# Conditioning columns off two projections' ends, the second block's shifts on VectorE, and the step widths' chain behind a convolution's taps

## The chip, the cores and the metric

The kernel runs as one program on one core of one Trainium2 chip. Its time is the device time of one execution in microseconds (us). TensorE (PE, matrix products), VectorE (DVE), ScalarE (ACT), GpSimd (POOL) and the queue of SyncE (SP), which issues the transfers, each run their own instruction stream in order and meet at semaphores. A stream that waits holds up all that stands behind it in the same stream.

## The reference, cut to what matters

Three blocks follow each other on 256 tokens of width 1024. The first has two layers (a state space mixer with a gated short convolution, then attention), each with a gated feed-forward network; the second is one recurrent mixer with a mixture of 32 experts; the third is an attention block. The diff touches three computations: the step widths `dt` of the state space mixer, the modulation rows `mod` that condition blocks two and three, and the shifted projections, decays and recurrence of the second block's mixer.

```python
# block 1, layer 1
xbc = silu(causal_dwconv(xbc, conv_w) + conv_b)
dt = softplus(dt_raw + dt_bias)
da = dt * -exp(a_log)
a_cs = cumsum(da)                      # decays follow from it
# block 2 (block 3 likewise, three parts of its own)
mod = silu(c) @ ada_w[l] + ada_b[l]
shift1, scale1, gate1, shift2, scale2, gate2 = split(mod, 6)
# block 2, mixer
zs = z + (z_prev - z) * mu             # token_shift; r, k, v are parts of zs
log_decay = -exp(-softplus(-w_pre) - 0.5)
kk = k * k_k / max(norm(k * k_k), eps)
k = k * (1 + (a - 1) * k_a)
for t in tokens:                       # per head
    state = state * w_t - (state @ kk_t) (kk_t * a_t)^T + v_t k_t^T
    y_t = state @ r_t
```

The kernel computes the recurrence in chunks of 128 tokens, which needs products of the decays with k, kk and r and the inverse of a triangular matrix for each chunk and head.

## The kernel before, in words

**Projections.** `dense_F` multiplies the 256 tokens by a weight matrix. Weights come as raw tiles through SP's queue and are worked off in units of 128 x 1024. Each unit is split into a high part `wh` (a rounded copy on ACT, line 338) and a low part `wl` (the difference, line 342, on DVE; every third unit of the first block's larger matrices on POOL). PE then runs 24 products of 128 x 256 for a unit: `xh*wh`, `xl*wh`, `xh*wl`, for eight groups. Units are split three ahead of PE (two ahead in the second block's mixer), and there are four buffers of `wh` and `wl` (three in the mixer). Four accumulators `acc` hold results.

**Background work.** Everything that isn't a projection is written as generators in one queue (`push`). `tick` runs the next piece of the first of them, and `dense_F` calls it once a unit. So the order in which all engines see the pieces is settled when the program is built: a piece stands, in every engine's stream, behind the splits of the units that were issued before it. `drain` runs what is left.

**Step widths.** After the 16 columns of `dt_raw` are projected, `widths` (line 868) transposes them on PE (L875), runs a softplus on DVE and ACT (L876 to L889, with Exp at L879 and Ln at L882), forms `da` (L890), and a tick later runs two products with it and two Exp (L896, L897). Before, it is pushed ahead of `conv(8)`, the first of three convolutions. Each convolution pushes 12 taps on DVE (L811) and a Silu on ACT (L814). `consts2` then builds masks on DVE and POOL.

**Conditioning columns.** One column of `mod` is one DVE instruction over a 128 x 1024 tile `adat` of transposed `ada_w` (`cond`, L1274), which multiplies by `silu(c)` and sums. There are 56 columns, and three `adat` buffers. Each column, when it is done, issues the transfer of a later column's tile (`cond_load`, L1291). `MODS[i]` says how many columns are pushed at which place in layer i's feed-forward network: entry 2q after gate product q, entry 2q+1 after up product q (q from 0 to 5), entry 11 + k/4 at unit k of the down product. The residual `sg` of gate and up is multiplied at L1161, split at L594, and the down product reads it.

**Second block's mixer.** `shift` (L1390) forms token-shifted r, k and v: one difference, on POOL for the wide ones (L1392), then four fused multiply-adds on DVE (L1394). `k_chain` and `r_chain` multiply them with decays (`KR` at L1462 and L1477, `v["k"]` with `E2` at L1478). In `rwkv`, `invert` solves 15 steps on DVE for each half t (L1693 to L1697), `Tm` is formed from it (L1780), and `corner` (L1771) masks `AB` on POOL. Four transposes per group (L1787) and products follow.

Of the kernel before, what the change touches and what calls it, by code (L numbers as in the profile page):

```python
# [33 lines left out]
T = 256  # L34
# [112 lines left out]


EXPERTS = [(1, 0)] + [x for e in range(31) for x in ((1, e + 1), (2, e))] + [(2, 31)]
MODS = [[0, 3] + [2] * 9 + [3] + [0] * 6, [0, 3] + [2] * 9 + [3] + [3, 3, 2, 0, 0, 0]]  # L150


def weight_plan(stages):
# [271 lines left out]
class KB:  # L425
# [351 lines left out]
    def ssd_layer(self, xf):  # L777
        nc, pp = self.nc, self.pp
        es = ExitStack()
        P = es.enter_context(self.pool("ssd", 1))  # L780
        X = self.xpool

        warm = self.tl(pp, [128, 128], F32, "tp")
        for _ in range(8):
            self.mm(warm, self.ident, self.ident, start=True)
        self.st.ahead(1)
        x = self.resplit(xf, X)

        def padded(n):
            pad = self.tl(P, [128, 4, T + 3], F32, "pad", bufs=2)  # L790
            nc.gpsimd.memset(pad[:, :, 0:3], 0.0)
            return pad


        xs = self.tl(P, [128, 8, T], F32, "xs")
        bc = self.tl(P, [128, 4, T], F32, "bc")

        def conv(c0):
            ps = self.dense_F("w_in_mix", x)
            pad = padded(4)  # L800
            dst = xs[:, c0:c0 + 4] if c0 < 8 else bc
            for j in range(4):
                if j % 2 == 0:
                    nc.scalar.activation(pad[:, j:j + 2, 3:], ps[j // 2], AF.Copy)
                nc.scalar.activation(dst[:, j], ps[j // 2][:, j % 2], AF.Identity, bias=self.col("conv_b", c0 + j),
                                     scale=self.col("conv_w", 36 + c0 + j))

            def taps():
                for j in range(4):
                    for tap in range(3):  # L810
                        nc.vector.scalar_tensor_tensor(dst[:, j], pad[:, j, tap:tap + T], self.col("conv_w", 12 * tap + c0 + j),  # L811
                                                       dst[:, j], op0=OP.mult, op1=OP.add)
                    yield
                nc.scalar.activation(dst, dst, AF.Silu)  # L814

            self.push("conv", taps())

        self.x_done = False
        ps = self.dense_F("w_in_mix", x, n=16)
        dr = self.tl(P, [16, T], F32, "dr")  # L820
        nc.scalar.activation(dr, ps[0][0:16, 0], AF.Copy)
        v = {}
        self.push("widths", self.widths(P, dr, v))
        conv(8)
        self.push("consts", self.consts2())
        conv(0)
        conv(4)
        self.push("states", self.state_space(P, xs, bc, v))

        z = self.z = self.tl(P, [128, 8, T], F32, "z")  # L830
        for h in range(2):
            ps = self.dense_F("w_in_mix", x)
            for j in range(2):
                s = slice(4 * h + 2 * j, 4 * h + 2 * j + 2)
                nc.scalar.activation(z[:, s], ps[j], AF.Silu)

        self.pad(P, 16)
        sx = (self.tl(P, [128, 8, T], F32R, "sch"), self.tl(P, [128, 8, T], F32R, "scl"))
        for h in range(2):
            cc = self.tl(P, [128, 4, T], F32, "cc")  # L840
            ps = self.dense_F("w_in_mix", x)
            for j in range(2):
                nc.scalar.activation(cc[:, 2 * j:2 * j + 2], ps[j], AF.Copy)
            ps = self.dense_F("w_in_mix", x)
            pad = padded(4)
            for j in range(2):
                nc.vector.tensor_mul(pad[:, 2 * j:2 * j + 2, 3:], cc[:, 2 * j:2 * j + 2], ps[j])
            for j in range(4):
                c = h * 4 + j
                nc.scalar.activation(cc[:, j], pad[:, j, 3:3 + T], AF.Copy, scale=self.col("sc_w", 16 + c))  # L850
                for tap in range(2):
                    nc.vector.scalar_tensor_tensor(cc[:, j], pad[:, j, 1 + tap:1 + tap + T], self.col("sc_w", 8 * tap + c),
                                                   cc[:, j], op0=OP.mult, op1=OP.add)
            ps = self.dense_F("w_in_mix", x)
            for j in range(2):
                s = slice(2 * j, 2 * j + 2)
                nc.vector.tensor_mul(cc[:, s], cc[:, s], ps[j])
                so = slice(4 * h + 2 * j, 4 * h + 2 * j + 2)
                self.split(cc[:, s], sx[0][:, so], sx[1][:, so])
        self.x_done = True  # L860
        ps = self.residual(xf)
        self.rows_T("w_out_mix", sx, 0, 8, ps)
        self.drain()
        r = self.rows_norm("w_out_mix", self.yx, 8, ps, "lnm", 0, self.cond_fill(0))
        es.close()
        return r
# [485 lines left out]
    def mixer(self, xf, stat):  # L1352
        nc, pp, st = self.nc, self.pp, self.st
# [11 lines left out]
        c4 = lambda ap: ap.rearrange("p j (t s) -> p j t s", s=128)  # L1365
# [23 lines left out]

        def shift(pad, mu0, n, dst):  # L1390

            (nc.gpsimd if n > 2 else nc.vector).tensor_sub(dst, pad[:, 0:n, 0:T], pad[:, 0:n, 1:])  # L1392
            for j in range(n):
                nc.vector.scalar_tensor_tensor(dst[:, j], dst[:, j], self.col("mu", mu0 + j), pad[:, j, 1:],  # L1394
                                               op0=OP.mult, op1=OP.add)

        KR = self.tl(P, [128, 4, 2, 2, 128], F32, "KR")
        bz = self.tl(P, [128, 2, 4, T], F32, "bz")
        ta, sig, cs, E1, g = t4("d"), t4("a"), t4("b"), t4("c"), t4("e")
        E0, E2 = sig, cs  # L1400
        hs = self.tl(P, [128, 4], F32, "hs")
        v = {}
# [41 lines left out]
        def k_chain(pad):  # L1444
            zk = v["k"] = t4("f")
            shift(pad, 4, 4, zk)
            yield
            kap, sq = t4("h"), t4("i")
            for j in range(4):
                nc.vector.tensor_scalar(kap[:, j], zk[:, j], self.col("k_k", j), None, op0=OP.mult)  # L1450
            nc.scalar.activation(sq, kap, AF.Square)
            yield
            rs = self.head_rsqrt(sq, P, 1.0, 1e-24, OP.max)
            yield
            for j in range(4):
                nc.vector.tensor_mul(kap[:, j], kap[:, j], self.head_row(rs, j))

            f = t4("i")
            for j in range(4):
                nc.scalar.activation(f[:, j], ta[:, j], AF.Identity, bias=hk[:, 1, j:j + 1], scale=hk[:, 0, j:j + 1])  # L1460
            yield
            nc.gpsimd.tensor_mul(KR[:, :, :, 0], c4(kap), c4(E0))  # L1462
            nc.vector.scalar_tensor_tensor(ta, ta, 1.0, kap, op0=OP.add, op1=OP.mult)
            nc.vector.tensor_mul(zk, zk, f)
            yield

            for e in range(2):
                nc.vector.scalar_tensor_tensor(bz[:, e], ta, hm[:, e:e + 1], E2, op0=OP.mult, op1=OP.mult)
            yield

        def r_chain(pad):
            zr, sq = t4("h"), t4("i")
            shift(pad, 0, 4, zr)
            yield
            for j in range(4):
                nc.vector.scalar_tensor_tensor(sq[:, j], zr[:, j], self.col("r_k", j), v["k"][:, j], op0=OP.mult, op1=OP.mult)
            nc.vector.tensor_mul(KR[:, :, :, 1], c4(zr), c4(E1))  # L1477
            nc.gpsimd.tensor_mul(v["k"], v["k"], E2)  # L1478
            v["bonus"] = sq
            yield  # L1480

# [32 lines left out]
        pad = padded(ps, 2)  # L1514
# [116 lines left out]
    def rwkv(self, P, P2, KR, bz, kh, V, hs, stick):  # L1631
# [136 lines left out]
        TT = self.tl(P, [128, 2, 8, 128], F32, "bz")  # L1768
        Al = {}

        def corner(lev, t):  # L1771
            Al[t] = self.tl(P, [128, 8, 128], F32, "pad", bufs=2)
            nc.gpsimd.tensor_mul(Al[t], units(AB[:, t, :, :, 0:128]), self.corners[:, lev, None, :].to_broadcast([128, 8, 128]))

        for t in range(2):
            corner(0, t)
        for t in range(2):
            for _ in inv[t]:
                pass
            nc.vector.tensor_mul(  # L1780
                Tm[:, t].rearrange("p u (b s) -> p u b s", s=16), Tc[:, t, :, None, :].to_broadcast([128, 8, 8, 16]),
                self.blk16.rearrange("p (b s) -> p b s", s=16)[:, None].to_broadcast([128, 8, 8, 16]))
        for t in range(2):
            for h in range(2):
                p = self.tl(pp, [128, 4, 128], F32, "tp")
                for u in range(4):
                    nc.tensor.transpose(p[:, u], Tm[:, t, 4 * h + u], self.ident)  # L1787
                nc.scalar.activation(TT[:, t, 4 * h:4 * h + 4], p, AF.Copy)
            fill()
# [842 lines left out]
```

## Time and profile before

| | us |
|---|---|
| three executions | 2259.61, 2260.05, 2253.85 |
| their median | 2259.61 |
| the profiled execution | 2253.87 |
| its span, first to last instruction | 2252.1 |
| PE busy in it | 2122.8 (94%) |
| DVE, ACT, POOL busy | 1073.3, 724.5, 269.1 |

The mean granted clock of PE was 0.974 of its full speed. The profile gives busy time by engine and by 40 slices of the span, then groups of instructions by line. The trace can be asked for the waits of an engine, for a stretch of the timeline, and for the busy time in given windows. In a timeline row the first number is the start in us from the start of the span, the second the duration; a bracket at its end gives the idle time of the engine just ahead and what ended it. A row with "x6" is a run of six instructions of one kind.

### The profile page before, as it was taken

Reading aid. Unit: us, or ns where it says so; the run is one execution under the profiler, and the core shown is the slowest. Engines: PE = TensorE matmul, PEld = TensorE weight load, DVE = VectorE, ACT = ScalarE, POOL = GpSimd, SP = SyncE. Lnnn points to the kernel's source line nnn. Section 1 sums busy time; section 2 is a strip of 40 time slices with the busy share of each in tenths; the row PEclk is TensorE's granted clock in tenths of the full one; section 3 lists DMA queues with packets and bytes.
Section 4 is the critical chain, followed back from the end, with each engine's and each line's share of the span. In section 5 each row is a group of like instructions: output and inputs, shape, how many; then the busy total and the mean of one; then the engine's idle time right before and its main releaser. Section 6 shows DMA issues by size and latency. Waiting matters only on the chain. (4 is left out here: it accounts for less than half of the span.)

```text
span 2252.1 us, 31704 instructions
## 1 busy us (share of the span) xinstructions
PE 2122.8 (94%) x13258; PEld 1489.4 (66%) x13258; DVE 1073.3 (48%) x2013; ACT 724.5 (32%) x1169; POOL 269.1 (12%) x144
## 2 busy tenths in 40 slices
PE   8999999999999988799899999999999999999996
PEld 8997997887997878688444444334433333368886
DVE  6775775566787567746222222322221111245665
ACT  5444543554543454343111110111111111133552
POOL 2322232100232012310000000000000000004101
PEclk9999999999999999999899999999999999999999
DMA  7334785332787433105799999999999999984320
GB/s 295 150 146 158 309 315 206 152 150 86 312 319 271 176 122 113 38 1 219 324 426 427 427 423 427 427 428 427 427 428 427 428 427 427 427 333 161 119 76 20
DMA packets 65652, 618.06 MB, mean 274 GB/s; under 512 B 8128, under 2 KB 10176, under 8 KB 19808
## 3 DMA queue, kind: packets, MB, share of 16 engines
q1 hardware_dynamic: 62320, 612.33, 66.5%
q10 hardware_dynamic: 3184, 3.65, 0.5%
q8 instruction: 106, 1.74, 0.3%
q14 instruction: 42, 0.34, 0.0%
HBM read 614.90 MB, written 1.05 MB: 274 GB/s over the span
## 5 line engine op out<-in xcount | busy, mean ns | idle before, releaser
L555 PE MATMUL acc<-xh,wh 128*128 128x256 f32 (+1 forms) x1736 | 487.5, 285 | 7.3 <-ACT wh L338 2.8
L555 PE MATMUL acc<-xl,wh 128*128 128x256 f32 (+1 forms) x1736 | 482.2, 281 | 2.9 <-DVE xl L594 1.5
L555 PE MATMUL acc<-xh,wl 128*128 128x256 f32 (+2 forms) x1704 | 476.4, 280 | 5.3 <-DVE wl L342 5.3
L555 PE MATMUL acc<-expert,xe 128*64 128x512 f32 x2000 | 447.7, 598 | 17.7 <-DMA expert<-exp_w 17.7
L342 DVE TENSOR_TENSOR wl<-w,wh 128x1024 fp32r<-128x1024 f32 x202 | 270.1, 1346 | 155.3 <-ACT wh L338 154.8
L338 ACT ACTIVATE wh<-w 128x1024 fp32r<-128x1024 f32 (+1 forms) x263 | 274.0, 1054 | 213.7 <-PE acc L555 176.0
L555 PEld LDWEIGHTS acc<-xh,wh 128*128 128x128 f32 (+1 forms) x1736 | 326.5, 189 | 16.2 <-issue 5.6
L555 PEld LDWEIGHTS acc<-expert,xe 128*64 128x64 f32 x2000 | 140.5, 137 | 294.8 <-issue 275.5
L555 PEld LDWEIGHTS acc<-xl,wh 128*128 128x128 f32 (+1 forms) x1736 | 328.8, 191 | 7.5 <-DVE xl L594 3.5
L555 PEld LDWEIGHTS acc<-xh,wl 128*128 128x128 f32 (+2 forms) x1704 | 322.5, 189 | 7.1 <-DVE wl L342 6.9
L555 PE MATMUL py<-expert,aT 128*64 128x512 f32 x1024 | 234.3, 600 | 3.6 <-DMA expert<-exp_w 2.8
L342 POOL TENSOR_TENSOR wl<-w,wh 128x1024 fp32r<-128x1024 f32 (+1 forms) x61 | 153.4, 2515 | 527.6 <-ACT wh L338 468.4
L2069 ACT ACTIVATE s<-a 128x512 f32<-128x512 f32 x32 | 20.2, 630 | 530.1 <-DVE a L2068 530.1
L2136 DVE SCALAR_TENSOR_TENSOR xf<-py,mod,xf 128x256 f32<-128x256 f32 x128 | 55.7, 479 | 279.8 <-PE py L555 279.8
L2068 DVE TENSOR_SCALAR a<-acc 128x512 f32<-128x512 f32 x32 | 22.1, 692 | 346.2 <-PE acc L555 346.2
L555 PEld LDWEIGHTS py<-expert,aT 128*64 128x64 f32 x1024 | 72.0, 138 | 137.3 <-issue 127.8
L342 POOL TENSOR_TENSOR wl<-w_w_in,wh 128x1024 fp32r<-128x1024 f32 (+1 forms) x11 | 26.8, 2435 | 1053.8 <-ACT wh L338 1042.9
L1274 DVE SCALAR_TENSOR_TENSOR adat<-adat,pe 128x1024 f32<-128x1024 f32 x56 | 97.3, 1756 | 12.3 <-DMA adat<-tiles 12.3
L2123 ACT ACTIVATE y<-py 64x512 f32<-64x512 f32 x64 | 37.9, 592 | 117.9 <-PE py L555 117.4
L555 PE MATMUL tp<-sel,xh 128*128 128x128 f32 x512 | 63.3, 284 | 7.9 <-ACT aT L2103 6.9
L555 PE MATMUL acc<-wh,hh 128*128 128x512 f32 x176 | 69.7, 396 | 0.0
L555 PE MATMUL acc<-wl,hh 128*128 128x512 f32 x176 | 69.4, 394 | 0.0
(641 smaller groups left out, 2856.2 us busy)
## 6 DMA issues: line engine op xcount, KB each, us to landing
expert<-exp_w SPq DMA_DIRECT2D x188, 2048.0 KB, 31.3
w<-tiles SPq DMA_DIRECT2D x140, 1024.0 KB, 6.9
adat<-tiles SPq DMA_DIRECT2D x56, 512.0 KB, 7.7
w_w_in<-tiles SPq DMA_DIRECT2D x18, 1024.0 KB, 5.0
w<-exp_w SPq DMA_DIRECT2D x3, 2048.0 KB, 7.6
w_w_out<-tiles SPq DMA_DIRECT2D x4, 1024.0 KB, 4.8
expert<-exp_w SPq DMA_DIRECT2D x4, 512.0 KB, 30.1
w_w_o_moba<-tiles SPq DMA_DIRECT2D x2, 1024.0 KB, 4.7
```

The costliest lines, as they stand in the source:

```text
L338: kb.nc.scalar.activation(hi, w, AF.Copy)
L342: (kb.nc.gpsimd if far else kb.nc.vector).tensor_sub(lo, w, hi.bitcast(F32))
L555: self.nc.tensor.matmul(out, lhsT, rhs, start=start, stop=True, skip_group_check=True)
L1274: self.nc.vector.scalar_tensor_tensor(w, w, 1.0, crow[:, int(m >= 48)], op0=OP.mult, op1=OP.mult, accum_out=dst)
L2068: nc.vector.tensor_scalar(a, pg, 7.0, None, op0=OP.min)
L2069: nc.scalar.activation(s, a, AF.Sigmoid, scale=1.702)
L2123: nc.scalar.activation(y[r, o], py[r], AF.Copy)
L2136: nc.vector.scalar_tensor_tensor(xf[:, k], ps[o][:, c], gate2(k), xf[:, k], op0=OP.mult, op1=OP.add)
```

## The change

Four places are edited. The step widths' generator is pushed behind the first convolution's taps. The table `MODS` has three columns instead of two after gate 2, up 3 (and the same in layer 2), none after gate 5 and up 5, and three at unit 4 of the down product (layer 2: 3, 3, 3, 2 from there). The wide shift differences, the first half of `KR` and the product of k with `E2` go from POOL to DVE. The first two of the `corner` masks go from POOL, ahead of the inversion's last steps, to DVE, right behind each `Tm`.

```diff
-MODS = [[0, 3] + [2] * 9 + [3] + [0] * 6, [0, 3] + [2] * 9 + [3] + [3, 3, 2, 0, 0, 0]]
+MODS = [[0, 3, 2, 2, 3, 2, 2, 3, 2, 2, 0, 0] + [3] + [0] * 5, [0, 3, 2, 2, 3, 2, 2, 3, 2, 2, 0, 0] + [3, 3, 3, 2, 0, 0]]
...
         v = {}
+        conv(8)
         self.push("widths", self.widths(P, dr, v))
-        conv(8)
         self.push("consts", self.consts2())
...
-            (nc.gpsimd if n > 2 else nc.vector).tensor_sub(dst, pad[:, 0:n, 0:T], pad[:, 0:n, 1:])
+            nc.vector.tensor_sub(dst, pad[:, 0:n, 0:T], pad[:, 0:n, 1:])
...
-            nc.gpsimd.tensor_mul(KR[:, :, :, 0], c4(kap), c4(E0))
+            nc.vector.tensor_mul(KR[:, :, :, 0], c4(kap), c4(E0))
...
-            nc.gpsimd.tensor_mul(v["k"], v["k"], E2)
+            nc.vector.tensor_mul(v["k"], v["k"], E2)
...
-        def corner(lev, t):
+        def corner(lev, t, engine=nc.gpsimd):
             Al[t] = self.tl(P, [128, 8, 128], F32, "pad", bufs=2)
-            nc.gpsimd.tensor_mul(Al[t], units(AB[:, t, :, :, 0:128]), self.corners[:, lev, None, :].to_broadcast([128, 8, 128]))
-
-        for t in range(2):
-            corner(0, t)
+            engine.tensor_mul(Al[t], units(AB[:, t, :, :, 0:128]), self.corners[:, lev, None, :].to_broadcast([128, 8, 128]))
+
         for t in range(2):
             for _ in inv[t]:
                 pass
             nc.vector.tensor_mul(
...
+            corner(0, t, nc.vector)
```

What this does to the instruction streams is shown at three places. The numbers behind names count tiles as the program makes them, and differ between the two kernels.

ACT, from the first units of layer 1's input projection, kernel before:

```order
L821 ACTIVATE dr_189<-acc_149 16x256
L338 ACTIVATE wh_193<-w_1_76 128x1024
L879 ACTIVATE dw_37_225<-dw_37_225 128x32
L880 ACTIVATE na_231<-rows_96 128x16
L882 ACTIVATE dw_39_227<-dw_38_226 128x32
L338 ACTIVATE wh_250<-w_4_79 128x1024
L896 ACTIVATE dte_230<-tp_278 128x16
L897 ACTIVATE ea_229<-tp_278 128x16
```

The same four lines of the step widths in the changed kernel, now behind the Silu of the first convolution:

```order
L338 ACTIVATE wh_455<-w_3_78 128x1024
L814 ACT_TABLE_LOAD
L814 ACTIVATE bc_148<-bc_148 128x1024
L879 ACT_TABLE_LOAD
L879 ACTIVATE dw_59_488<-dw_59_488 128x32
L880 ACTIVATE na_494<-rows_96 128x16
L882 ACT_TABLE_LOAD
L882 ACTIVATE dw_61_490<-dw_60_489 128x32
L338 ACTIVATE wh_513<-w_5_154 128x1024
L896 ACT_TABLE_LOAD
L896 ACTIVATE dte_493<-tp_541 128x16
L897 ACTIVATE ea_492<-tp_541 128x16
```

The chain now has a table load ahead of its Exp, another ahead of its Ln and a third ahead of the later Exp; ACT's stream has four loads more in all, the fourth ahead of a later Silu (L835). On PE the two products with `da` stand 192 products, eight units, later than before.

DVE, at the end of layer 1's up product, where the residual is multiplied (L1161), kernel before:

```order
L1274 SCALAR_TENSOR_TENSOR adat_3580,mod_15_119<-adat_3580,pe_2344 128x1024
L342 TENSOR_TENSOR wl_3745<-w_30_3297,wh_3744 128x1024
L1274 SCALAR_TENSOR_TENSOR adat_3611,mod_15_119<-adat_3611,pe_2344 128x1024
L1274 SCALAR_TENSOR_TENSOR adat_3708,mod_15_119<-adat_3708,pe_2344 128x1024
L1161 TENSOR_TENSOR sg_3741<-sg_3741,acc_3743 128x512
L594 TENSOR_TENSOR hl_2349<-sg_3741,hh_2348 128x512
L342 TENSOR_TENSOR wl_3830<-w_30_3297,wh_3829 128x1024
```

The same place in the changed kernel:

```order
L1274 SCALAR_TENSOR_TENSOR adat_3586,mod_15_119<-adat_3586,pe_2344 128x1024
L342 TENSOR_TENSOR wl_3751<-w_30_3300,wh_3750 128x1024
L1161 TENSOR_TENSOR sg_3747<-sg_3747,acc_3749 128x512
L594 TENSOR_TENSOR hl_2349<-sg_3747,hh_2348 128x512
L342 TENSOR_TENSOR wl_3830<-w_30_3300,wh_3829 128x1024
L342 TENSOR_TENSOR wl_3849<-w_31_3429,wh_3848 128x1024
```

The two columns that stood between the last `wl` and L1161 are gone from there; three stand some units later, in the down product.

DVE, at the end of the inversion of the first half, kernel before:

```order
L1695 TENSOR_REDUCE k_9059<-k_9059 128x8
L1697 TENSOR_SCALAR k_9059<-k_9059,idc_596 128x8
L1780 TENSOR_TENSOR kz_9369<-k_9059,blk_77_599 128x1024
L1697 TENSOR_SCALAR k_9059<-k_9059,idc_596 128x8
L1693 TENSOR_TENSOR k_9059<-k_9059,bz_9178 128x8x12
```

The same place in the changed kernel, whose lines there have numbers lower by two:

```order
L1695 TENSOR_REDUCE k_9059<-k_9059 128x8
L1697 TENSOR_SCALAR k_9059<-k_9059,idc_624 128x8
L1778 TENSOR_TENSOR kz_9369<-k_9059,blk_79_627 128x1024
L1773 TENSOR_TENSOR pad_9373<-AB_9046,corners_628 128x1024
L1697 TENSOR_SCALAR k_9059<-k_9059,idc_624 128x8
L1693 TENSOR_TENSOR k_9059<-k_9059,bz_9178 128x8x12
```

The corner mask stands between the first half's `Tm` (L1780, now L1778) and the rest of the second half's inversion.

## Rows read from the trace of the kernel before

**Rows 1.** Page, busy us by engine (share of the span, instructions):

```profile
PE 2122.8 (94%) x13258; PEld 1489.4 (66%) x13258; DVE 1073.3 (48%) x2013; ACT 724.5 (32%) x1169; POOL 269.1 (12%) x144
```

**Rows 2.** Waits of PE: tile, line waited for: us, times, longest:

```profile
PE acc L555 <- DVE sg L1161: 11.1, 2, 5.6
...
PE tp L1497 <- DVE k L1394: 4.0, 1, 4.0
PE tp L1787 <- DVE k L1697: 3.7, 1, 3.7
...
PE tp L555 <- DVE da L890: 3.0, 1, 3.0
```

**Rows 3.** Windows: us, busy by engine (instructions), granted clock, DMA share, GB/s:

```profile
23.00:26.25 3.25, 3.25 (x17) 3.25 (x16) 0.00 (x0) 0.56 (x1) 2.38 (x2) 0.50 1.02 416
26.25:58.50 32.25, 32.25 (x286) 32.25 (x286) 27.37 (x58) 22.71 (x32) 9.78 (x9) 1.00 0.56 220
358.70:364.20 5.50, 5.48 (x17) 4.71 (x18) 4.21 (x6) 1.58 (x2) 0.00 (x0) 0.50 0.51 171
695.80:699.00 3.20, 3.19 (x12) 2.95 (x13) 2.29 (x3) 1.57 (x2) 0.00 (x0) 0.54 0.48 165
957.40:964.50 7.10, 7.07 (x25) 5.22 (x25) 5.68 (x17) 2.52 (x5) 0.00 (x0) 0.50 0.00 0
```

**Rows 4.** Timeline, end of layer 1's up product, DVE and PE:

```profile
356.83 1.23 DVE L1274 SCALAR_TENSOR_TENSOR adat<-adat,pe 128x1024 f32<-128x1024 f32 x1 [3.71 <-DMA adat<-tiles]
...
357.98 0.68 DVE L1161 TENSOR_TENSOR sg<-sg,acc 128x512 f32<-128x512 f32 x1
...
358.72 1.65 PE L555 MATMUL acc<-alphaI,xf 128*128 128x128 f32 x6 [5.61 <-DVE sg L1161]
```

**Rows 5.** Tile `adat`, 255 to 375 us, its 21 transfers:

```profile
DMA to landing us min/median/max: 3.5/7.7/10.4
```

**Rows 6.** Timeline, layer 1's input projection, ACT, DVE and PE:

```profile
18.58 0.23 ACT L879 ACTIVATE dw<-dw 128x32 f32<-128x32 f32 x1 [2.92 <-DVE dw L878]
...
20.70 0.19 DVE L890 SCALAR_TENSOR_TENSOR da<-dt,na 128x32 f32<-128x32 f32 x1
...
42.26 1.28 ACT L814 ACT_TABLE_LOAD   x1
...
43.55 1.06 ACT L814 ACTIVATE bc<-bc 128x1024 f32<-128x1024 f32 x1
...
60.69 0.39 PE L555 MATMUL acc<-xh,wl 128*128 128x256 f32 x1 [1.71 <-DVE wl L342]
```

**Rows 7.** Timeline, second block's mixer, PE and DVE:

```profile
843.91 2.16 PE L555 MATMUL tp<-heads,i 128*128 128x2 f32 x16 [2.07 <-ACT i L1451]
...
853.96 3.43 DVE L1463 SCALAR_TENSOR_TENSOR d<-d,h 128x1024 f32<-128x1024 f32 x1
...
869.11 1.21 DVE L1477 TENSOR_TENSOR KR<-h,c 128x1024 f32<-128x1024 f32 x1
...
875.54 1.67 DVE L1394 SCALAR_TENSOR_TENSOR k<-k,cols,pad 128x256 f32<-128x256 f32 x4 [4.08 <-POOL k L1392]
```

**Rows 8.** Timeline, inversion and first transposes, POOL, DVE and PE:

```profile
945.84 2.35 POOL L1773 TENSOR_TENSOR pad<-AB,corners 128x1024 f32<-128x1024 f32 x1 [14.98 <-PE tp L555]
...
946.40 1.96 DVE L1697 TENSOR_SCALAR k<-k,idc 128x8 f32<-128x8 f32 x2
...
953.88 3.42 DVE L1780 TENSOR_TENSOR kz<-k,blk 128x1024 f32<-128x1024 f32 x1
...
957.43 1.94 PE L1787 MATMUL tp<-ident,kz 128*128 128x128 f32 x8 [3.70 <-DVE k L1697]
...
964.50 1.29 PE L1787 MATMUL tp<-ident,kz 128*128 128x128 f32 x8
```

**Rows 9.** Page, GB/s moved in 40 equal slices of the span:

```profile
GB/s 295 150 146 158 309 315 206 152 150 86 312 319 271 176 122 113 38 1 219 324 426 427 427 423 427 427 428 427 427 428 427 428 427 427 427 333 161 119 76 20
```

**Rows 10.** Timeline, SP's queue, first expert transfers of the mixture:

```profile
1042.96 21.00 SPq L412 DMA_DIRECT2D expert<-exp_w  x6
```

## The prediction

> **What bounds the kernel now.** I began with the page's busy times: PE works 2122.8 of 2252.1 us [rows 1], so the time is PE's work plus its idle time, 129 us in all, plus what a lower clock adds. The change takes nothing from PE's work. It can only act on idle time and clock, so the second view was PE's waits by what ended them: 11.1 us in two waits for the residual product at L1161, 4.0 for the shift at L1394, 3.7 for the inversion's L1697, 3.0 for the step widths' L890 [rows 2]. All four are places of the diff. The third view was the windows behind such waits: the granted clock stands at 0.50 to 0.54 there (the 1.2 GHz level), where the stretch 26.25 to 58.50 shows 1.00 (2.4 GHz) [rows 3]. So a wait costs its idle time and then half, or nearly, of a slow stretch: 3.25 x 0.50 = 1.6 us behind the widths, 5.50 x 0.50 = 2.75 and 3.20 x 0.46 = 1.5 behind the two residuals. The timeline (rows 4 and 6 to 8) then gives what stood ahead of each wait in the waiting engine's stream. In 26.25 to 58.50 PE needs 32.25 us for 286 products, 0.113 each; a unit of 24 takes 2.7.
>
> **Conditioning columns (B).** At 356.83 a column on DVE waits 3.71 for its `adat` tile, and the gate multiply L1161 stands behind it in DVE's stream and starts at 357.98. PE's residual needs the accumulators that L1161 frees and is idle for 5.61 [rows 4]. Layer 2 repeats it: the two waits of [rows 2] sum to 11.1, so 5.5 there. In the new order L1161 stands directly behind the last `wl`. DVE does then what it did, less the column. Removed are 11.1 of idle and 2.75 + 1.5 of slow clock, 15.3. What stays is the time that L1161 itself takes behind the last product, 0.68 [rows 4], of which PE sees about 0.4 a layer, since other accumulators are still free. The term is -14.5. Bounds: -15.3 if nothing stays; -8 if the wait for L1161 is still 1.5 in each layer and the slow clock comes all the same (2 x 4.0 of idle gained, none of clock).
>
> The columns aren't dropped. Two per layer move to gate 2 and up 3, and three to unit 4 of the down product, 1.2 us of DVE each. Nothing waits for them there but later columns. A column issues the transfer for the column three after it, and one column runs per unit. At the old place four columns ran in four successive units (gate 5 and up 5 have two units each), so a tile had 3 x 2.7 = 8.2 us. With three columns after a product of four units the third column back is always four units back, 10.9 us, and a tile lands 3.5 to 10.4 us after its issue, median 7.7 [rows 5]. SP's queue, past which they move, carries the same transfers in the same number. I cost this at nothing; its cover is DVE's lead of some units, and rival 4 is the price without it.
>
> **Step widths (A).** Before, the chain's Exp starts at 18.58 and L890 ends at 20.89, 2.31 us [rows 6]; PE waits 3.0 [rows 2] and then runs slow, 1.6: together 4.6 to be gained. At the new place the products with `da` stand 192 products later. PE reaches them (in the old trace's clock, from about 21.5) after 192 x 0.113 + 1.6 = 23.3, at 44.8; the two transposes that move with the chain make it 45.2. ACT ends the Silu of the taps at 43.55 + 1.06 = 44.6. Only then comes the new table load for Exp, 1.28 (the length at 42.26 [rows 6]): 45.9. From Exp to the end of L890 it is 2.31 again, and the load ahead of Ln adds 1.28: 49.5. PE waits 49.5 - 45.2 = 4.3 and runs slow again: 1.5 to 2.75 by the three stretches of [rows 3], I take 2.0. So 6.3 is added. One thing goes: at 60.69 PE waits 1.71 for a `wl` [rows 6] that stood behind masks and taps on DVE, and that stands ahead of the last masks now. Sum -4.6 + 6.3 - 1.7 = 0. The two further table loads (ahead of L896 and of a later Silu) take 2 x 1.28 on ACT, which is busy for 22.7 of 32.25 us there [rows 3] and splits three units (8.2 us) ahead; nothing is late. Bounds: -2 without a slow stretch, +3 with the longer one and the 1.71 still there.
>
> By the Trainium skill, page "ScalarE: Activation LUTs", section "What ACT_TABLE_LOAD costs", a switch takes 1283 ns of load and 1380 ns of drain, 2.66 us. The trace agrees with the load, 1.28; of the drain it shows nothing behind the load, since the Silu starts 0.01 us after it. With the page's 2.66 for each of the two loads in the chain, A would by that estimate be +2.8 instead of 0.
>
> **Shifts, KR and E2 on DVE (C).** Five instructions of 128 x 1024 go from POOL to DVE at the 1.21 of L1477 [rows 7]: +6.1 us of DVE. DVE is relieved of two things. Its two-input instructions stretch while POOL works: L1463 takes 3.43 against 1.21 for its like, so 2.2 go. And it waits 4.08 at 875.54 for POOL's difference of L1392 [rows 7], where its own would take 1.2, so 2.9 go. That leaves +1.0 on DVE over the mixer. On PE: the k chain ends 1.2 later, so the idle time at 843.91, behind L1451 of that chain, grows from 2.07 to about 3.2. At 877 the wait of 4.0 for L1394 [rows 2] comes to the same end, the difference being no longer late but DVE having the added work ahead of it: 0 to -1.2. Sum 0. Bounds: -4.0 if that wait goes wholly, +4.5 if the added 6.1 less half of the relief (2.5 of 5.1), and the 1.2 at 843.91 less what overlaps, show on PE.
>
> **Corners on DVE (D).** POOL's corner at 945.84 runs beside L1697 at 946.40, a pair of which takes 1.96; the next one runs beside `Tm` at 953.88, which takes 3.42 [rows 8] instead of the 1.21 of a like instruction [rows 7], 2.2 too much. L1697 works on 128x8, and L890 on 128x32 takes 0.19 [rows 6], so a pair needs under 0.4; 1.6 go. PE waits 3.70 for this chain at 957.43, and is slow until 964.50 [rows 3, 8]; the DVE corner adds 2 x 1.2 on the same stream, the first ahead of the second half's last steps, the second behind `Tm`. Chain: -2.2 - 1.6 + 1.2 = -2.6 for the first transposes, and as less idle time also means less of the 7.10 x 0.50 = 3.55 of slow clock, of which I take 2.2 back, -4.8. Bounds: -2 (chain alone, and a little lost) and -5.5 (the chain and nearly all of the slow stretch).
>
> **Sum.** -14.5 + 0 + 0 - 4.8 = -19.3. What lies ahead of the mixture of experts moves up as a whole, and the experts' transfers with it: the first are issued at 1042.96 [rows 10], behind all four places. The profiled execution took 2253.87, so 2234.6 in its terms. It is as low as the lowest of the three runs and 5.7 below their median, 2259.61; I put the forecast half of that higher, at **2237**.
>
> **Rivals.**
>
> 1. Table switches are dearer than 1.28 (A). ACT must empty before a load: one full-size instruction of 1.06 [rows 6] for each of the two loads in the chain, 2.1, and the third load, 1.28, comes onto the path of `dte`: +3.4, **2240**. For it: three loads where there was none. Against: the Silu that starts 0.01 us behind its load. By the figures of the Trainium skill's page named above, an estimate of +2.8, it is 2240 as well. Chance 0.12.
>
> 2. C isn't hidden (+4.5), and of D only 2.0 comes: -14.5 + 4.5 - 2.0 = -12.0, **2245**. For it: DVE's chains end the waits in both places, so added work there is at once on the path. Against: the stretched 3.43 and the wait of 4.08, which pay for most. Chance 0.12.
>
> 3. The gain is given back in the mixture of experts. From the 21st slice on transfers run at 423 to 428 GB/s for 15 slices [rows 9], so that stretch is as long as its bytes. If the start at 1042.96 [rows 10] doesn't move with PE, all is lost: no change, 2254 to **2259**. Against: those six issues stretch over 21 us [rows 10], as issues do that wait for something the engines free. Chance 0.06.
>
> 4. Slower: the tiles of the three-column groups come late. If landing takes longer than 10.9 us behind issue, each of six groups of three (gate 2, up 3 and the down product, two layers) waits as 356.83 does: 5.5 of idle and about 2.1 of slow clock, 7.6, six of them 46. With the other terms, 2237 + 46 - about 5 for groups that DVE's lead covers, **2278**. It decides from a landing of 10.9 plus that lead; the longest now is 10.4 [rows 5], and the old place shows a wait of 3.7 with 8.2 us to land, so the margin is thin. Against: products of four units leave DVE time. Chance 0.04.
>
> The forecast, terms as summed, has the rest, 0.66.
>
> **How the numbers follow.** The terms' bounds sum to -26.8 (-2 - 15.3 - 4 - 5.5) and -2.5 (+3 - 8 + 4.5 - 2), but not all at one end: 2227 is the low end (half of the low bounds' excess below 2234.6), and the high end is 2249, which takes in rivals 1 and 2 with 5 us of scatter; outside are rivals 3 and 4 and some more. A measurement of this kernel tells 0.3%, 6.8 us, from no change, so faster means under 2252.8. Forecast and rivals 1 and 2 are faster but for the slow tail of rival 2: 0.88. Rival 3 and that tail: 0.08. Rival 4: 0.04.
>
> **What would show it.** B: no wait of PE for L1161 over 1 us, clock 1.00 behind both residuals, no column waiting over 1 us at gate 2 and up 3. A: a wait of PE for `da` of about 4.3 eight units later, three loads of 1.28 in the chain, slow clock behind it; the wait for `wl` at about 60 gone. C: no instruction of L1463's kind over 1.3, PE's wait at L1451 about 3.2. D: `Tm` at 1.2, transposes' wait near 1. The forecast is wrong if waits for L1161 stay (then B is below 8), if columns wait for tiles at new places, or if the first expert transfer is not about 19 earlier than 1042.96.

## The result, and the profile after

| | before | after |
|---|---|---|
| median of five executions, us | 2259.61 | 2244.13 |
| lowest and highest | 2253.85, 2260.44 | 2239.66, 2248.96 |
| the profiled execution | 2253.87 | 2248.96 |
| its span, granted clock | 2252.1, 0.974 | 2247.0, 0.971 |

The ratio is 0.9938, with a 95% interval of 0.9919 to 0.9958: faster by 9 to 18 us. The two profiled executions differ by 4.9 only, since the one of before is the lowest of its five and the one of after the highest. So the profiles are compared place by place. For that I took the same ACT instruction in both traces, one that follows a certain projection product, and subtracted its starts:

| ACT instruction | start before | shift after | what lies between |
|---|---|---|---|
| L804, first convolution | 27.50 | -5.92 | widths' wait gone from its old place |
| L804, third convolution | 49.26 | +2.27 | widths at the new place |
| L843, short convolution | 88.01 | +3.27 | state space part begins |
| L593 `sch`, last | 168.15 | +11.92 | state space part |
| L593 `hh` in layer 1 | 341.70 | +12.12 | |
| L338 behind the residual | 389.71 | +3.66 | first residual: -8.5 |
| L338 in layer 2 | 684.90 | +4.40 | |
| L338 behind its residual | 706.61 | -2.73 | second residual: -7.1 |
| L1498, mixer | 877.84 | -4.01 | shifts, KR, E2: -1.3 |
| L1914, mixer | 1002.45 | -7.33 | corners: -3.3 |
| L338, third block | 2204.49 | -7.22 | |
| L2519, last | 2238.24 | -4.86 | |

In this pair of profiles three of the four places went as their terms say, or nearly; the widths cost 12 us where I had nothing. The page and PE's waits after, which answer to [rows 1, 2]:

```profile
PE 2130.6 (95%) x13258; PEld 1499.2 (67%) x13258; DVE 1074.6 (48%) x2020; ACT 729.8 (32%) x1173; POOL 253.4 (11%) x137
```

```profile
PE tp L555 <- DVE da L890: 4.0, 1, 4.0
...
PE py L555 <- DVE M L966: 3.4, 1, 3.4
...
PE tp L555 <- ACT i L1451: 3.4, 1, 3.4
PE tp L555 <- POOL sg L942: 3.3, 1, 3.3
...
PE tp L928 <- ACT Bt L917: 2.5, 1, 2.5
...
PE tp L1497 <- DVE k L1394: 2.2, 1, 2.2
...
PE tp L1787 <- DVE kz L1778: 2.0, 1, 2.0
```

The 11.1 for L1161 are not in the list any more. Three waits of the state space part stand near the top now: for `M`, `sg` and `Bt`, 9.2 us. PE's work is the same, and its busy time is 7.8 us longer: the same products took longer. The fall of the mean granted clock from 0.974 to 0.971 is by itself about 7 of some 2250 us. Windows of after (us, busy by engine, granted clock, DMA share, GB/s) answer to [rows 3]:

```profile
42.50:51.50 9.00, 7.87 (x42) 7.90 (x43) 4.95 (x21) 3.98 (x6) 0.48 (x1) 0.62 0.55 189
84.50:88.50 4.00, 3.87 (x22) 3.87 (x23) 2.94 (x3) 1.97 (x3) 0.00 (x0) 0.61 1.01 424
118.50:123.50 5.00, 4.88 (x33) 4.55 (x34) 4.37 (x8) 0.00 (x0) 0.97 (x1) 0.67 0.91 383
137.00:147.00 10.00, 6.78 (x38) 6.23 (x39) 6.29 (x8) 2.25 (x4) 5.14 (x3) 0.66 0.54 211
360.00:366.00 6.00, 6.00 (x56) 6.00 (x55) 4.46 (x6) 2.44 (x3) 3.18 (x1) 1.00 0.93 381
694.00:700.00 6.00, 6.00 (x35) 5.21 (x34) 1.90 (x3) 1.45 (x2) 0.00 (x0) 1.00 0.97 355
949.00:958.50 9.50, 8.81 (x34) 6.98 (x35) 8.76 (x20) 3.49 (x8) 0.00 (x0) 0.52 0.01 3
```

Behind both residuals PE has no idle time and full clock. In layer 1's mixer there are four slow stretches (busy time times the missing clock: 3.0, 1.5, 1.6 and 2.3 us) where before had one, behind the widths. The first shows the chain as predicted, with the loads in ACT's stream (timeline, ACT and PE), which answers to [rows 6]:

```profile
37.63 1.06 ACT L814 ACTIVATE bc<-bc 128x1024 f32<-128x1024 f32 x1
38.71 1.28 ACT L879 ACT_TABLE_LOAD   x1
40.00 0.23 ACT L879 ACTIVATE dw<-dw 128x32 f32<-128x32 f32 x1
...
40.36 1.28 ACT L882 ACT_TABLE_LOAD   x1
41.65 0.23 ACT L882 ACTIVATE dw<-dw 128x32 f32<-128x32 f32 x1
...
43.63 0.58 PE L555 MATMUL tp<-da,gt 128*128 128x16 f32 x2 [3.98 <-DVE da L890]
```

The last is a place on which the prediction says nothing (timeline, POOL and PE):

```profile
136.36 2.36 POOL L342 TENSOR_TENSOR wl<-w,wh 128x1024 fp32r<-128x1024 f32 x1 [10.63 <-ACT wh L338]
138.68 3.46 POOL L942 TENSOR_TENSOR sg<-gt,da 128x512 f32<-128x512 f32 x2
...
140.22 2.08 PE L555 MATMUL tp<-lower,sg 128*128 128x128 f32 x8 [3.33 <-POOL sg L942]
```

An `sg` for PE stands on POOL behind a `wl`. The three waits of the state space part in the kernel before, for comparison (timeline, PE):

```profile
79.37 0.66 PE L928 MATMUL tp<-ident,xs 128*128 128x128 f32 x4 [1.07 <-ACT Bt L917]
...
116.17 0.66 PE L555 MATMUL py<-M,xdt 128*64 128x128 f32 x8 [2.71 <-DVE M L966]
...
134.57 1.16 PE L555 MATMUL tp<-lower,sg 128*128 128x128 f32 x8 [0.26 <-POOL sg L942]
```

They sum to 4.0, against 9.2 after. On POOL the program now has one `sg` fewer ahead of a `wl` and one more behind it, because the state space part starts one unit later: counted in the traces, its first products on PE stand behind 528 projection products, where they stood behind 504.

### The profile page after: what moved, and what is told of

It is laid out like the page before. It is cut to its first block, busy times and chain, and to the rows that moved or that the text cites. A ratio compares the mean times of both kernels' runs of the same rounds, so it can differ in the third digit from the quotient of the medians.

```text
span 2247.0 us, 31704 instructions
## 1 busy us (share of the span) xinstructions
PE 2130.6 (95%) x13258; PEld 1499.2 (67%) x13258; DVE 1074.6 (48%) x2020; ACT 729.8 (32%) x1173; POOL 253.4 (11%) x137
## 3 DMA queue, kind: packets, MB, share of 16 engines
HBM read 614.90 MB, written 1.05 MB: 274 GB/s over the span
## 5 line engine op out<-in xcount | busy, mean ns | idle before, releaser
L338 ACT ACTIVATE wh<-w 128x1024 fp32r<-128x1024 f32 (+1 forms) x263 | 273.9, 1054 | 212.6 <-PE acc L555 172.7
L342 DVE TENSOR_TENSOR wl<-w,wh 128x1024 fp32r<-128x1024 f32 x202 | 262.1, 1307 | 146.3 <-ACT wh L338 145.6
L1274 DVE SCALAR_TENSOR_TENSOR adat<-adat,pe 128x1024 f32<-128x1024 f32 x56 | 103.5, 1868 | 5.1 <-DMA adat<-tiles 4.7
```

The costliest lines, as they stand in the source:

```text
L338: kb.nc.scalar.activation(hi, w, AF.Copy)
L342: (kb.nc.gpsimd if far else kb.nc.vector).tensor_sub(lo, w, hi.bitcast(F32))
L1274: self.nc.vector.scalar_tensor_tensor(w, w, 1.0, crow[:, int(m >= 48)], op0=OP.mult, op1=OP.mult, accum_out=dst)
```

## The experiments

After the result I held **theory 1**: the move of the widths (A in the prediction; B are the columns, C the shifts, D the corners) costs about 12 us, because in the background queue all that follows them starts one unit later, and so the waits of the state space part grow. Its rivals: the table loads are the cost; or nothing is, and the profiled execution only had more slow clock. Ratios are to the kernel before in the same job; shifts are those of the last L593 `sch` in layer 1's mixer (168.15 before). In five profiles whose kernel has neither the move nor the other queue (before and the runs e1, e5, e6 and e7 below) that shift lies between -0.8 and +3.3; so much is chance.

**e1_bcd**, all but A:

```diff
-        conv(8)
         self.push("widths", self.widths(P, dr, v))
+        conv(8)
```

> The changed kernel with the step widths put back ahead of the first convolution (A undone; columns, mixer and corners as changed). Theory 1: A costs about 12 us, as the starts of the same instructions in the two profiles say (0 before the widths, +11.9 behind layer 1's mixer). Then this runs at about 2232, and PE's waits in layer 1's mixer are those of the kernel before: 3.0 for the widths, 2.7 and 0.3 in the state space part. Rival: A is worth nothing, as I forecast, and the profiled execution was only one with more slow clock; then it stays at 2240 to 2248.

Measured: 2239.97, ratio 0.9917 (0.9899 to 0.9935), shift +2.4. PE's waits there are 3.0 for the widths, 2.8, 0.8 and 0.3, as before. By the median it is 4.2 us faster than the changed kernel, of an expected 12, which is where the rival had it, and the two intervals overlap: the times alone don't settle what A costs in company of the rest. In the two profiles the difference is 9.5 at the last `sch` and 4.9 at the last row of the table; e1 lost the rest further on, most of it between 1002 and 2204, which the edit doesn't touch.

**e2_a**, A alone on the kernel before:

```diff
+        conv(8)
         self.push("widths", self.widths(P, dr, v))
-        conv(8)
```

> The kernel before with A alone. Theory 1: slower by 8 to 12 us (ratio about 1.004 to 1.005), with PE's waits of 4.0 for the widths, 2.5, 3.4 and 3.3 in the state space part. Rival (A is worth nothing): ratio 1.000, within 2 us.

Measured: 2270.00, ratio 1.0049 (1.0033 to 1.0066), which is 7 to 15 us slower, and a shift of +11.8. The waits are 4.0, 2.2, 3.4 and 3.3. A alone costs time; that rival is out.

**e3_bcd_y**, all but A, and two empty steps in the widths:

```diff
         yield
+        yield
+        yield
         pc = self.tl(pp, [128, 2, 16], F32, "tp")
```

> As the run without A, and the step widths in their old place, but with two empty steps between the softplus and the two products with da, so that the products stand two units later and still within the first convolution's product. If the wait of 3.0 and the slow stretch behind it (1.6) are worth what the rows say, another 4 to 5 us go against the run without A: about 2228. If the work only waits elsewhere, it equals the run without A.

Measured: 2235.60, ratio 0.9898 (0.9880 to 0.9916), shift -1.0. PE's wait for the widths is gone. About 3 of the 4 to 5 us show in the trace against e1, within what is chance; the rest returns at a `wl` behind the masks on DVE, where e1 has no wait:

```profile
57.95 0.39 PE L555 MATMUL acc<-xh,wl 128*128 128x256 f32 x1 [2.90 <-DVE wl L342]
```

This version beats both kernels: its interval lies below that of the changed one. It overlaps that of e1, so the gain of the two steps isn't shown by the times, and 2235.60 is not the 2228 expected.

**e4_silu**, the chain ahead of the Silu, so without the three table loads:

```diff
+                if c0 == 8:
+                    yield from self.widths(P, dr, v)
                 nc.scalar.activation(dst, dst, AF.Silu)
...
-        self.push("widths", self.widths(P, dr, v))
```

> The changed kernel with the widths' chain between the last tap and the Silu of the first convolution, so that ACT has no table load ahead of its Exp, Ln and later Exp. The state space part still starts one step later in the background queue than before. If the table loads are what A costs, the waits in the state space part (2.5, 3.4, 3.3) go with them and it runs 8 to 12 us below the changed kernel, 2234. If the one step is, only the wait of 4.0 for the widths goes, with the slow stretch behind it: 4 to 6 below, about 2239, and the later waits stay.

Measured: 2246.04, ratio 0.9943 (0.9924 to 0.9962), shift +7.1 against the changed kernel's +11.9. The widths' wait is 1.8 instead of 4.0, and the later waits of 2.5, 3.4 and 3.3 stay. So the waits of the later start stay without the loads, as theory 1 has it. The shift is 4.8 smaller, hardly more than the 4 us of chance, and the edit does two things: it drops the loads, and it takes the chain ahead of the Silu. What the loads alone cost isn't shown. The times don't tell e4 from the changed kernel; the profiled execution lost 3.8 in layer 1's feed-forward network, which the edit doesn't touch (last section).

**e8_tick**, an empty step in the queue of the kernel before:

```diff
+        self.push("pad", iter([None]))
         self.push("consts", self.consts2())
```

> The kernel before with nothing moved but one empty step in the background queue, between the first convolution's taps and the masks: the state space part starts one unit later, as it does with A, and there is no table load more. Theory 1 (the later start costs): PE's waits in the state space part become 2.5, 3.4 and 3.3 as with A, with slow clock behind them, and from 86 to 168 us the start of the same instructions shifts by about +8; time +5 to +9, ratio about 1.003. Rival (the table loads or the place of the chain cost it): waits as before (1.1, 2.7, 0.3), no shift.

Measured: 2267.53, ratio 1.0023 (1.0009 to 1.0036), shift +4.9. The waits became 2.2, 3.4 and 3.3 with the widths untouched (waits of PE, 15 to 160 us; lines there have numbers higher by one):

```profile
PE py L555 <- DVE M L967: 3.4, 1, 3.4
PE tp L555 <- POOL sg L943: 3.3, 1, 3.3
PE tp L555 <- DVE da L891: 3.0, 1, 3.0
PE tp L929 <- ACT Bt L918: 2.2, 1, 2.2
```

The later start alone makes them: the part's first products stand behind 528 projection products here too. From L843 to the last `sch` the shift grows by 5.3, not by about 8, because behind the wait for `sg` the clock stayed at 1.00 here (windows as above):

```profile
114.00:120.00 6.00, 5.00 (x34) 4.67 (x35) 5.25 (x8) 0.00 (x0) 1.84 (x2) 0.72 0.87 345
136.50:147.00 10.50, 10.45 (x94) 9.74 (x96) 6.71 (x11) 3.69 (x5) 3.86 (x2) 1.00 0.47 193
```

Up to layer 1's residual another 3.8 is lost without a new wait of PE, at the slower rate of products that the last section shows. So not all of the longer time has to be these waits.

**e5_b, e6_c, e7_d**, one part each on the kernel before: the new table of columns; the three edits from POOL to DVE; the two corners.

```diff
-MODS = [[0, 3] + [2] * 9 + [3] + [0] * 6, [0, 3] + [2] * 9 + [3] + [3, 3, 2, 0, 0, 0]]
+MODS = [[0, 3, 2, 2, 3, 2, 2, 3, 2, 2, 0, 0] + [3] + [0] * 5, [0, 3, 2, 2, 3, 2, 2, 3, 2, 2, 0, 0] + [3, 3, 3, 2, 0, 0]]
```

> The kernel before with the new table of columns alone (B). From the profile after: -8.5 at layer 1's residual and -7.1 at layer 2's, -15.6 in all, about 2243, ratio 0.993. The rival that half of it depends on the other parts: 2250.

Measured: 2243.27, ratio 0.9912 (0.9886 to 0.9937); the shift falls by 8.5 at the first residual and 7.1 at the second. B doesn't depend on the others, and alone it is as fast as the whole change: the intervals overlap, and its median is 0.9 lower.

```diff
-            (nc.gpsimd if n > 2 else nc.vector).tensor_sub(dst, pad[:, 0:n, 0:T], pad[:, 0:n, 1:])
+            nc.vector.tensor_sub(dst, pad[:, 0:n, 0:T], pad[:, 0:n, 1:])
...
-            nc.gpsimd.tensor_mul(KR[:, :, :, 0], c4(kap), c4(E0))
+            nc.vector.tensor_mul(KR[:, :, :, 0], c4(kap), c4(E0))
...
-            nc.gpsimd.tensor_mul(v["k"], v["k"], E2)
+            nc.vector.tensor_mul(v["k"], v["k"], E2)
```

> The kernel before with the mixer's five instructions on DVE alone (C). From the profile after: +2.1 at the products behind L1451, then -3.4 at the transposes behind L1394, -1.3 in all: no difference that the times can tell (ratio 0.999 to 1.000), and these two shifts in the trace. Rival of the prediction: +4.5.

Measured: 2261.92, ratio 1.0001 (0.9987 to 1.0014). In the trace 2.1 us go between 814 and 878.

```diff
-        for t in range(2):
-            corner(0, t)
...
+            corner(0, t, nc.vector)
```

> The kernel before with the two corners on DVE alone (D). From the profile after: about -3.3 between 930 and 980 us, ratio 0.9985; the prediction had -4.8. PE's wait for the transposes about 2.0 instead of 3.7, and the slow clock as long as before if it follows any such wait, or shorter if its length goes with the wait.

Measured: 2261.60, ratio 1.0001 (0.9986 to 1.0016). In the trace 3.0 us go between 937 and 988, and PE's wait is 1.97. The times show no gain from either part: D's 3 us would be at the very end of its interval, C's 2 are within. Nor is e1, which has B, C and D, faster than B alone. That C and D help rests on the traces alone.

**e9_masks and e10_masks_a**, the masks moved out of layer 1's mixer, so that the state space part starts earlier; e9 is e3 with this, e10 the changed kernel with this. Beside the lines shown, the masks get a scratch tile of their own and one `iota` more on POOL.

```diff
-        self.push("consts", self.consts2())
...
             self.ada_end += sum(MODS[i])
+        if i == 0:
+            self.push("consts", self.consts2(P))
```

> As the run with the step widths in their old place and two empty steps, and the masks (consts2) moved from the first convolutions into layer 1's feed-forward network, with a scratch tile of their own. The state space part then starts three steps earlier, and some 10 us of DVE leave the second and third convolution. If the place of that part in the queue sets its waits, the wait of 2.9 for wl at 58 and the waits of 2.7 and 0.3 in the state space part go, with their slow clock: about 2228. If they only move to other pieces, or the masks hold up columns in the feed-forward network, it stays at 2235.

> The changed kernel (A in) with the masks moved in the same way: the state space part is two to three units earlier than in the changed kernel, the widths' chain stays behind the taps with its three table loads. If A costs through the later start of the state space part, its later waits (2.5, 3.4, 3.3) go and only the wait of 4.0 for the widths and its slow clock stay: about 2234 to 2236. If the table loads or the chain's place itself are all of A's cost, it stays near the changed kernel, 2242 to 2244.

Measured: e9 2240.26, ratio 0.9916 (0.9903 to 0.9930), shift -0.8; e10 2243.28, ratio 0.9924 (0.9910 to 0.9937), shift -1.9. In e10 the widths' wait is 4.0 as in the changed kernel, the waits for `Bt` and `sg` are gone, that for `M` is 3.1 (waits of PE, 15 to 160 us):

```profile
PE tp L557 <- DVE da L891: 4.0, 1, 4.0
PE py L557 <- DVE M L967: 3.1, 1, 3.1
```

The shift of +11.9 has become -1.9: A's later cost hangs on when the state space part starts, as theory 1 has it (the masks' own work has left DVE there too, which this run doesn't separate). The time of e10 doesn't follow; it is where the rival had it. By the shifts 8.4 are lost again before layer 1's residual, where PE now waits 2.78 at 265.45 for a `wl` that stands behind the masks, with slow clock behind, and the products run at the slower rate (last section). e9 missed: `wl` at 58 waits no more, but `M` waits 4.5, and the masks cost 2.8 at 264.92 with slow clock behind; it isn't faster than e3.

## Why the prediction was right or wrong

The time lies in the range, faster as forecast, 7 us above the forecast of 2237. The sum is off by one term. With that term as measured, +11.9, the forecast would have been 2249, the very end of the range; that the median falls inside, at rival 2's number and not by rival 2's mechanism, is luck. The range itself holds a slip: half of the low bounds' excess would give 2231, and 2227 is all of it.

**B, right.** -14.5 was forecast, and the shifts give -8.5 - 7.1 = -15.6. L1161 waits for PE alone now (timeline of DVE, answers to [rows 4]), and PE for nothing:

```profile
360.72 1.21 DVE L342 TENSOR_TENSOR wl<-w,wh 128x1024 fp32r<-128x1024 f32 x1
362.59 0.69 DVE L1161 TENSOR_TENSOR sg<-sg,acc 128x512 f32<-128x512 f32 x1 [0.65 <-PE acc L555]
```

I had left 0.4 a layer for that; it is nothing. Rival 4, late tiles, did not come: landing takes 10.4 at most, as in [rows 5], and the columns wait 1.4 us in all in layer 1, their longest wait there, 1.05, standing in the kernel before as well (1.17 at 267.50).

```profile
DMA to landing us min/median/max: 4.6/7.6/10.4
```

**A, the step that failed: "Sum -4.6 + 6.3 - 1.7 = 0".** Measured +11.9 in the profile after, +11.8 with A alone. The terms of the moved step are near: 5.9 gained at the old place (4.6 forecast; kernels without an edit there are shifted by -1.9 to +0.2 at that point), a wait of 3.98 (4.3), a slow stretch of 3.0 (2.0). The -1.7 for the `wl` at 60.69 was no term of the change. The wait is gone after, but it is gone in e1 and e6 too, where nothing ahead of it was edited. It came where this `wl` on DVE ran beside a `wl` on POOL and took 3.40, as before (first fence), and not where it took 1.22, as in e1 (second; timeline of DVE):

```profile
57.23 3.40 DVE L342 TENSOR_TENSOR wl<-w,wh 128x1024 fp32r<-128x1024 f32 x1
```

```profile
57.74 1.22 DVE L342 TENSOR_TENSOR wl<-w,wh 128x1024 fp32r<-128x1024 f32 x1
```

What is missing is all that stands behind the widths in the queue. I counted what the moved step itself issues and not that every later piece runs one unit later, while the units that POOL splits stay the same. The state space part then waits 9.2 instead of 4.0 us (2.5, 3.4, 3.3 against 1.07, 2.71 and 0.26), and lost 1.5 + 1.6 + 2.3 more to the clock. The empty step in e8 shows this without the move, e10 the reverse. Why `sg` waits is seen on POOL; for `M` and `Bt` the runs show that the later start lengthens the waits, and what stands ahead of them is open. From L843 to the last `sch` the shift grows by 8.7 in the profile after, by 5.3 in e8. The other 3.3 are there by L843, where e4 has -1.1; how much of them is the loads stays open. Alone A costs 11 us, beside the other parts 4 by the medians; why the parts don't add up isn't shown.

**Rival 1** named the right edit with the wrong cause. Each load takes 1.28, the first two with 0.01 to 0.02 us of idle time on either side. The third isn't on the path: it ends at 44.12, and the Exp behind it waits for PE until 44.67. What the page "ScalarE: Activation LUTs" of the Trainium skill adds in "What ACT_TABLE_LOAD costs", a drain of 1380 ns per switch, doesn't show here: ACT goes from Silu to load to Exp without a gap.

**C, right in its steps.** The timeline of DVE after answers to [rows 7]:

```profile
854.42 1.22 DVE L1463 SCALAR_TENSOR_TENSOR d<-d,h 128x1024 f32<-128x1024 f32 x1
...
871.59 1.67 DVE L1394 SCALAR_TENSOR_TENSOR k<-k,cols,pad 128x256 f32<-128x256 f32 x4
```

L1463 takes 1.22 instead of 3.43, L1394 waits for POOL no more, and PE's wait behind L1451 grew from 2.1 to 3.4 (3.2 forecast). Its wait for L1394 fell from 4.0 to 2.2, a little more than the 1.2 that I allowed: -1.3 in the profile after, -2.1 alone, for a forecast of 0. Rival 2's +4.5 did not come.

**D, the clock's part too large.** `Tm` and the corner behind it take 1.22 each (timeline of DVE, answers to [rows 8]):

```profile
948.32 1.22 DVE L1778 TENSOR_TENSOR kz<-k,blk 128x1024 f32<-128x1024 f32 x1
949.46 1.22 DVE L1773 TENSOR_TENSOR pad<-AB,corners 128x1024 f32<-128x1024 f32 x1
```

The chain gave its 2.6; the 2.2 that I took back from the slow clock did not come. PE's wait fell to 1.97, not to near 1, and its clock is at 0.52 over 949 to 958.5 all the same. So -3.3 instead of -4.8.

**Rival 3** is out: the first expert transfers are issued 7.2 earlier than in [rows 10], and the shift, -7.3 ahead of the mixture, is still -7.2 at 2204. That they are not about 19 earlier is a sign of being wrong that the prediction named, and it came (SP's queue after):

```profile
1035.77 44.38 SPq L412 DMA_DIRECT2D expert<-exp_w  x8
```

The parts sum to 11.9 - 15.6 - 1.3 - 3.3 = -8.3, which with +1.0 in unchanged places is the -7.3 of the trace up to the third block. The two profiled executions are the lowest of before and the highest of after, which is how I read the rest of the difference to the medians (14 us by the ratio).

## What to carry to other kernels

Where background pieces are advanced once per unit of work, moving one piece moves all behind it: look up what the later ones meet in each engine's stream, above all pieces that share an engine with the weights' splitting. Count a wait of TensorE with the slow stretch that may follow, which can nearly double it (3.70 and 3.55 at the transposes before). When an effect is smaller than the spread of executions, compare the start of the same instruction at several places of two traces; it tells where the time goes. How much of that is chance takes more than two: unedited places differed by 4 us here.

## What the runs showed of the hardware

**A wait of the same length is followed by slow clock or not.** At the end of the third block PE waits 2.56 in both kernels, whose code is the same there; the stretch behind has clock 1.00 before and 0.67 after. The first fence is of before, the second of after:

```profile
2215.30:2223.30 8.00, 4.68 (x39) 4.27 (x38) 6.52 (x7) 5.32 (x6) 2.69 (x1) 1.00 0.00 1
```

```profile
2208.00:2216.00 8.00, 4.98 (x24) 4.48 (x23) 6.52 (x7) 4.43 (x5) 2.66 (x1) 0.67 0.00 0
```

That is most of the 2.4 us between the last two rows of the table of shifts, and no effect of the change. Likewise the wait of 3.3 for `sg` has slow clock behind it in the profile after and none in e8.

**Products have two rates at full clock.** In the feed-forward networks PE is busy all the time with clock 1.00, and does 267 products of 128x256 in 30 us in some profiles and 257 in others; before and e3:

```profile
305.00:335.00 30.00, 30.00 (x267) 30.00 (x267) 23.84 (x25) 15.00 (x18) 10.13 (x4) 1.00 0.81 309
```

```profile
305.00:335.00 30.00, 30.00 (x257) 30.00 (x256) 23.29 (x27) 14.88 (x17) 7.20 (x3) 1.00 0.81 312
```

Of the twelve profiles six had the slower rate in layer 1 (e2, e3, e4, e8, e9, e10) and four in layer 2 (e1, e2, e3, e10). By the shifts it costs about 2 to 5 us a layer. What sets it is open. Each kernel has one profile, so nothing here shows that it changes between executions of one kernel. All six of layer 1 are kernels whose queue there was edited, and of the six others only the changed kernel is, so it may hang on the edits as well as on chance.
